# Issuing side work by a running account of engines, banks and buffers in a two-layer decoder trunk

## The chip, the cores and the metric

The kernel runs on one core of a Trainium2 chip. The metric is device time in microseconds (us), the median of three runs. The engines of the core are named as the profile names them: PE is TensorE's matmul, PEld its weight load, DVE is VectorE, ACT is ScalarE, POOL is GpSimd, and SP is SyncE, which here issues every DMA. Each engine works through its own queue in order, and waits for the others by semaphores.

## The reference

The input x is 256 tokens of 2048 channels, float32. Two residual layers, each behind an RMSNorm, are followed by a last RMSNorm.

```
for i in range(2):
    h = rms_norm(x, norm_w[i]); x = x + mixer_i(h)
return rms_norm(x, final_norm_w)
```

Mixer 0 is RWKV-7 time mixing. Six mixtures of h and its shifted copy are made; four go through the 2048 x 8192 projection (r, k, v, gate), two through small low-rank products (decay, learning rate). Each of 32 heads of 64 channels runs a recurrence over the tokens:

```
sa = S @ a_t
S = S * w_t + sa[..., None] * b_t + v_t[..., None] * k_t
y = S @ r_t
```

The result is normalized per head, gets a bonus (the head's sum of r*k*r_k, times v), is multiplied by SiLU of the gate and goes through a 2048 x 2048 output projection. Mixer 1 is differential attention: 16 heads, two causal softmax maps each with a distance penalty, the second subtracted with a learned weight, then values, a per-head RMS norm, the SiLU gate and an output projection.

## The kernel before

**The weight product.** Every projection is a run of `gemm` calls (line 229). A call has 8 steps (4 in the output projections); a step fetches 256 rows of 512 weight columns, splits them into a high half (`high`, a cast on ScalarE, `whi`) and the rest (`low`, a subtraction on VectorE, `wlo`), and multiplies three ways into two banks tagged `gm`. The split of a block is issued three steps ahead (LEAD). There are 320 such steps, in one written order: k, r, v, gate, output of the first layer, then the four projections of the attention layer in four groups, then its output. A layer's k, r, v and gate take 32 steps each; group j of a path is four pairs of heads.

**The side streams.** Everything else is written as Python generators that run while the kernel is built. After each step of the product, `gemm` calls `pump` (line 123), which first issues the waiting DRAM stores and then asks each live stream, in order of rank, for its next piece. A stream yields a price, an estimate of VectorE time. `pump` takes the next piece if VectorE's estimated lead over TensorE plus the price is within the rank's limit (`LIMITS`, line 37; the clocks are kept at lines 84 to 107). A negative price means that more pieces may be taken in the same call. `pump(True)` takes them regardless; it is called where the product can't go on without a stream (`until`, line 151). The order of issue is fixed when the program is built.

The streams of the first layer and their ranks are: scans 0; mixing, low-rank products, gates and `turns` 1; queries 2; keys 3; inverses 4; posts 5.

- `keys` (line 411) makes, for each of 16 pairs of heads, decays and scaled keys in bank `ka`, stores them to DRAM (`ppd`, `ard`, `bkd`) and builds a triangular block per chunk of 64 tokens. Each block takes two steps; the loads of the next are in one of them.
- `inverse` (line 486) inverts these blocks for two groups at once, with a long run of VectorE work (eight 32x32 transposes of 128x1024, 62 pairs of small instructions) and then four pieces of matmuls in banks `qa`.
- `query` (line 551) is called for each pair of heads, with its four chunks. It loads `rt`, `ppr`, `bkq` and `ard`, multiplies (VectorE), makes the score blocks in two `qa` banks and masks them (`G`, VectorE), then transposes in a third use of `qa` (copied out by ScalarE, line 588) and takes the bonus sums in a fourth. There are NR = 6 buffers for its results (`cont`, `G`); the first six run ahead and the others wait until the group that used the buffer is through (`C` marks).
- `scans` (line 610) walks 16 chunks (4 groups of 4) of all heads of a group: the copies `xsc` (lines 654, 655), a product with the inverse in bank `us` and the scaled result `uv` (VectorE), the state's update in `xy`, and the outputs in `ka`, copied by line 697. It needs the queries of the whole group (`Q` mark), the inverse of its pair of groups (`I`) and the values (`v`).
- `posts` (line 725) normalizes the outputs of a group, adds the bonus and applies the gate, on VectorE and some ScalarE. `turns` (line 781) transposes the result in `ka` for the output product.

The first output product starts behind `until("C3")` (line 916), the last chunk's copies; the second half of the output product needs the last `turns` (`until("T3")`, line 913).

## Time and profile before

| | us |
|---|---|
| median of 3 runs (1153.09 to 1157.58) | 1155.38 |
| the profiled execution | 1159.65 |
| its span | 1157.5 |
| PE busy | 1127.8 (97%) |
| DVE busy | 801.4 (69%) |
| ACT busy | 616.6 (53%) |

The first layer takes the span up to about 625 us, the attention layer the rest. A busy matmul row doesn't say that TensorE works at its peak, since matmuls overlap and their ends are modelled. So the profile is read by what TensorE waited for and by the length of a step of the product. A step is 12 matmuls of 512 columns or 24 of 256. Idle time of the other engines matters only where TensorE waits for them.

### The profile page before, as it was taken

What the parts mean: (1) busy time and instruction counts of PE and PEld (TensorE: products, weight loads), DVE (VectorE), ACT (ScalarE), POOL (GpSimd) and SP (SyncE); (2) the same over time, 40 slices, a digit from 0 to 9 for tenths busy, and PEclk for the clock granted to TensorE, in tenths of its full rate; (3) what the DMA queues carried; (4) which work ended last, traced back from release to release, by engine and by line L of the source; (5) the groups of instructions that cost most, each with busy time, mean ns of one, the idle gap of its engine ahead of it and who ended that gap; (6) DMA issues with size and microseconds to landing.
All of it is one profiled execution on the core that took longest, in us unless ns stands there. A gap on an engine that the chain in (4) does not pass through costs nothing.

```text
span 1157.5 us, 21930 instructions
## 1 busy us (share of the span) xinstructions
PE 1127.8 (97%) x8778; PEld 980.3 (85%) x8778; DVE 801.4 (69%) x1316; ACT 616.6 (53%) x1032; POOL 15.0 (1%) x38
## 2 busy tenths in 40 slices
PE   8999998999999989999999999999999999999996
PEld 6999998998777778877878899899889889987885
DVE  5755888988699668787796664476456647646764
ACT  7655854566543465455544543455456455545643
POOL 1010000000000000000001000000000000000000
PEclk9999999999999899999999999999999999999999
DMA  8646768876466557666575566655655665664463
GB/s 261 193 153 200 217 186 247 252 209 202 146 188 199 173 156 228 204 195 176 174 283 179 183 191 190 189 145 149 215 157 154 192 172 146 184 196 148 154 228 109
DMA packets 140823, 217.67 MB, mean 188 GB/s; under 512 B 29793, under 2 KB 45490, under 8 KB 140722
## 3 DMA queue, kind: packets, MB, share of 16 engines
q1 hardware_dynamic: 140722, 216.28, 62.1%
q8 instruction: 69, 1.13, 0.4%
q14 instruction: 32, 0.26, 0.1%
HBM read 197.37 MB, written 18.87 MB: 187 GB/s over the span
## 4 chain that ended last, share of the span: by engine, by line
PE 82%; DVE 9%; DMA 4%; issue 2%; ACT 2%; SPq 1%; ACTq 0%; DVEq 0%
PE gm L103 55%; PE us L103 14%; PE ka L103 7%; PE qa L103 4%; DVE wlo L95 3%; DVE itmp L95 1%; PE qa L107 1%; DVE wp L95 1%; DVE zp L95 1%; DMA wraw<-in_rwkv_w_out_dram 1%; DMA rd<-ev 1%; DMA bkq<-bkd 1%; DMA xin<-in_x_dram 1%; DMA uv<-vdr 1%; PE ka L107 1%
## 5 line engine op out<-in xcount | busy, mean ns | idle before, releaser
L95 DVE TENSOR_TENSOR wlo<-wraw,whi 128x1024 fp32r<-128x1024 f32 x320 | 389.1, 1222 | 118.2 <-ACT whi L196 117.5
L196 ACT CAST whi<-wraw 128x1024 fp32r<-128x1024 f32 x320 | 333.4, 1044 | 201.2 <-PE gm L103 136.1
L103 PE MATMUL gm<-whi,xs 128*128 128x512 f32 x944 | 324.4, 408 | 1.9 <-DVE acc L95 1.1
L103 PE MATMUL gm<-xs,whi 128*128 128x256 f32 x1376 | 256.3, 286 | 0.0
L103 PEld LDWEIGHTS gm<-whi,xs 128*128 128x128 f32 x944 | 180.2, 191 | 45.6 <-ACT whi L196 1.1
L103 PEld LDWEIGHTS gm<-xs,whi 128*128 128x128 f32 x1376 | 214.0, 189 | 3.5 <-issue 1.3
L103 PE MATMUL gm<-xs,wlo 128*128 128x256 f32 x688 | 194.8, 283 | 0.5 <-DVE wlo L95 0.5
L103 PE MATMUL gm<-wlo,xs 128*128 128x512 f32 x472 | 187.1, 396 | 0.0
L103 PEld LDWEIGHTS gm<-xs,wlo 128*128 128x128 f32 x688 | 129.6, 188 | 0.9 <-DVE wlo L95 0.9
L103 PEld LDWEIGHTS gm<-wlo,xs 128*128 128x128 f32 x472 | 90.5, 192 | 18.7
L103 PE MATMUL gm<-xt,whi 128*128 128x256 f32 x352 | 64.2, 283 | 0.0
L103 PE MATMUL gm<-whi,xt 128*128 128x512 f32 x176 | 58.1, 390 | 0.0
L103 PEld LDWEIGHTS gm<-xt,whi 128*128 128x128 f32 x352 | 53.7, 188 | 1.3 <-issue 1.3
L103 PE MATMUL gm<-xt,wlo 128*128 128x256 f32 x176 | 49.3, 280 | 0.0
L103 PEld LDWEIGHTS gm<-whi,xt 128*128 128x128 f32 x176 | 33.0, 188 | 7.6
L993 ACT ACTIVATE sc<-sc,mxx 128x128 f32<-128x128 f32 (+1 forms) x64 | 28.4, 445 | 18.1 <-DVE mxx L95 18.1
L103 PE MATMUL gm<-wlo,xt 128*128 128x512 f32 x88 | 34.7, 394 | 0.0
L95 DVE TENSOR_TENSOR xs<-ev,xs 128x512 fp32r<-128x512 f32 x32 | 22.1, 689 | 16.2 <-ACT xs L326 15.7
L103 PEld LDWEIGHTS gm<-xt,wlo 128*128 128x128 f32 x176 | 33.1, 188 | 0.0
L697 ACT COPY uv<-ka 64x512 f32<-64x512 f32 x16 | 9.3, 581 | 44.4 <-PE ka L103 44.4
L95 DVE SCALAR_TENSOR_TENSOR ev<-big,par,ev 128x256 f32<-128x256 f32 x64 | 28.0, 480 | 6.1 <-ACT ev L314 6.1
L314 ACT ACTIVATE ev<-big,omu 128x256 f32<-128x256 f32 x64 | 29.1, 502 | 5.8 <-DMA rd<-ev 3.9
(265 smaller groups left out, 1662.7 us busy)
## 6 DMA issues: line engine op xcount, KB each, us to landing
wraw<-in_rwkv_w_in_dram SPq DMA_DIRECT2D x128, 512.0 KB
wraw<-in_diff_w_in_dram SPq DMA_DIRECT2D x128, 512.0 KB
wraw<-in_rwkv_w_out_dram SPq DMA_DIRECT2D x32, 512.0 KB
wraw<-in_diff_w_out_dram SPq DMA_DIRECT2D x32, 512.0 KB
bkd<-bkc SPq DMA_DIRECT2D x16, 256.0 KB
bkq<-bkd SPq DMA_DIRECT2D x16, 256.0 KB
xin<-in_x_dram SPq DMA_DIRECT2D x4, 512.0 KB
kd<-ev SPq DMA_DIRECT2D x8, 256.0 KB
```

The source lines that it names most:

```text
L95: return fn(*args, **kw)
L103: PE.matmul(out, lhsT, rhs, start=start, stop=stop, **kw)
L107: PE.transpose(out=out, in_=in_, identity=identity)
L196: A.copy(his[i], raws[i])
L314: A.activation(m, ht[:, k, 1:T + 1], AF.Copy, scale=omu[:, col:col + 1])
L697: A.copy(ye, xyv[64:128].rearrange("p q h n -> p (q h n)"))
L993: A.activation(sc[:, m, b0:b1], sc[:, m, b0:b1], AF.Exp, bias=mx[:, t, m:m + 1], accum_out=sm[:, t, m:m + 1])
```

## The change

The two estimated clocks are replaced by an account (`given`) that follows PE, DVE, ACT, the SP queue and the DMA engines through every instruction as it is issued. It knows which part of which buffer each instruction reads and writes and when, by estimated durations, so an instruction starts in the account when its engine is free and its inputs are there and its output's former readers are done. Two DMAs that depend on each other through DRAM are not made to wait for each other. ACT and DVE instructions have new estimates, a 32x32 transpose 2.03 us.

A stream's next piece is issued only if everything that its last piece gave to other engines is due by TensorE's time plus `SLACK` (1 us), unless the price is negative. A piece may also name banks (`Ask`); their readers must be done by then too. Queries and scans name theirs. The limits become 8 for ranks 0 and 1, 6 for queries and posts, 5 for keys and inverses.

A query is made for one chunk of all four pairs of heads of a group, instead of one pair with its four chunks. Its loads take 64 tokens from each of four DRAM blocks. `r_k` moves from the product on VectorE into a small table `indk`. A scan chunk waits for its own query (`q` mark), and a query for the scan chunk that used its buffer six queries ago (`c` mark).

The post stage of a group may start while that of the group before is still under way, with buffers for two; the scale and shift are loaded once the group before is done.

```diff
+SLACK = 1.0
 BANKS = {"gm": 2, "ka": 2, "qa": 2, "xy": 1, "us": 1}
 LEAD = 3
 RAW = 4
 NR = 6
-LIMITS = (9, 9, 3, 4, 2.5, 3)
+LIMITS = (8, 8, 6, 5, 5, 6)
...
+    def after(table, k, box, eng, t):
+        for other, by, end in table.get(k, ()):
+            if by != eng and meets(box, other):
+                t = max(t, end + 0.07)
+        return t
+
+    def given(eng, cost, outs, ins):
+        t = free["sp" if eng == "dma" else eng]
+        outs, ins = [part(a) for a in outs] , [part(a) for a in ins]
+        for k, box in ins:
+            t = after(wrote, k, box, eng, t)
+        for k, box in outs:
+            t = after(seen, k, box, eng, after(wrote, k, box, eng, t))
+        if eng == "dma":
+            free["sp"] = t + 0.35
+            n = outs[0][1] if outs[0][1][1] > 1 else ins[0][1]
+            t = max(free["sp"] + 1.6, free["dma"])
+            cost = (n[1] - n[0]) * (n[3] - n[2]) * 4 / 240e3
+        end = t + cost
+        free[eng] = end
+        for k, box in outs:
+            wrote[k] = [w for w in wrote.get(k, ()) if not covers(box, w[0])] + [(box, eng, end)]
+            seen[k] = [r for r in seen.get(k, ()) if not covers(box, r[0])]
+        for k, box in ins:
+            seen[k] = [r for r in seen.get(k, ()) if not (r[1] == eng and covers(box, r[0]))] + [(box, eng, end)]
+        if eng != "pe":
+            late[0] = max(late[0], end)
...
+    V = Engine(nc.vector, "dve", 0.155, 0.00104)
+    A = Engine(nc.scalar, "act", 0.2, 0.00082)
+
+    class Queue:
+        def dma_start(self, dst, src):
+            given("dma", 0.0, [dst], [src])
+            nc.sync.dma_start(dst, src)
+
+    DMA = Queue()
...
     def mm(out, lhsT, rhs, start, stop, **kw):
-        n = math.prod(rhs.shape[1:]) * (1.0 if rhs.dtype == F32R else 4.0) / 2400
-        clock["pe"] += max(0.055, n)
+        n = math.prod(rhs.shape[1:])
+        if rhs.dtype == F32R:
+            cost = 0.231 * n / 512 if n > 256 else 0.118
+        else:
+            big_ = lhsT.shape[0] * math.prod(lhsT.shape[1:])
+            cost = 0.042 if big_ <= 1024 else 0.075 if big_ <= 8192 and n <= 64 else max(0.43 * n / 256, 0.21 if big_ > 8192 else 0.166)
+        given("pe", cost, [out], [lhsT, rhs])
         PE.matmul(out, lhsT, rhs, start=start, stop=stop, **kw)
...
+    class Ask(float):
+
+        def __new__(cls, price, *banks):
+            a = float.__new__(cls, price)
+            a.banks = banks
+            return a
+
+    def bank_free(tag, n):
+        k = turns_.get(tag, -1) + 1 + n
+        return max([0.0] + [end for _, by, end in seen.get((tag, k % BANKS[tag]), ()) if by != "pe"])
+
+    def timely(s):
+        if s[2] < 0:
+            return True
+        t = s[3]
+        banks = getattr(s[2], "banks", ())
+        for i, tag in enumerate(banks):
+            t = max(t, bank_free(tag, banks[:i].count(tag)))
+        return t <= free["pe"] + SLACK
+
+    def pump(any_=False):
         for dst, src, name in stores:
             DMA.dma_start(dst, src)
             done.add(name or "")
         stores.clear()
         for s in list(live):
-            while free or max(0.0, clock["dve"] - clock["pe"]) + abs(s[2]) <= LIMITS[s[0]]:
+            while any_ or (timely(s) and max(0.0, free["dve"] - free["pe"]) + abs(s[2]) <= LIMITS[s[0]]):
+                late[0] = 0.0
                 s[2] = next(s[1], None)
+                s[3] = late[0]
                 if s[2] is None:
                     live.remove(s)
                 if s[2] is None or s[2] >= 0:
...
+            asked = [c for c in price if c is not None]
+            yield Ask(sum(asked), *[b for c in asked for b in getattr(c, "banks", ())])
...
+    def query(j, c):
+        g, n = gs[j], j * NCH + c
+        if c == 0:
             g["G"], g["cont"] = [], []
             g["bon"] = L([P, NT, NPG, 2], "bon", 4)
-        rt = L([P, T], "rt", 1)
-        DMA.dma_start(rt, rd[j][q])
-        ppr = L([P, T], "ppr", 1)
-        DMA.dma_start(ppr, ppd[j][q])
-        bkc = L([P, NCH, 2, C], "bkq", 2)
-        DMA.dma_start(bkc.rearrange("p c e t -> p (c e t)"), bkd[j][q])
-        slot = b % NR
-        place, tag, n = (Y, "cont2", NR - 5) if slot > 4 else (S, "acc", 4) if slot else (L, "cont", 1)
-        cont = place([P, 2, NCH, P], tag, n)
-        ar = cont[:, 0].rearrange("p c (a t) -> p c a t", a=2)
-        DMA.dma_start(ar[:, :, 0, :], ard[j][q].rearrange("p (c t) -> p c t", c=NCH))
+        cs = slice(c * C, (c + 1) * C)
+        rt = L([P, NPG, C], "rt", 1)
+        DMA.dma_start(rt, rd[j][:, :, cs].rearrange("q p t -> p q t"))
+        ppr = L([P, NPG, C], "ppr", 1)
+        DMA.dma_start(ppr, ppd[j][:, :, cs].rearrange("q p t -> p q t"))
+        bkc = L([P, NPG, 2, C], "bkq", 2)
+        DMA.dma_start(bkc.rearrange("p q e t -> p q (e t)"),
+                      bkd[j][:, :, c * P:(c + 1) * P].rearrange("q p t -> p q t"))
...
+        V.tensor_tensor(ar[:, :, 1, :], rt, ppr, op=ALU.mult)
+        pr = L([P, NPG, C], "pr", 1)
+        V.tensor_tensor(pr, ar[:, :, 1, :], bkc[:, :, 1, :], op=ALU.mult)
+        yield Ask(1.5, "qa", "qa")
...
+        yield Ask(0.2, "qa", "qa")
         tp = I("qa")
...
+        s = slice(64 * (c % 2), 64 * (c % 2) + 64)
+        for q in range(NPG):
+            mm(bps[s, 2 * q:2 * q + 2], pr[:, q], indk[:, NPG * j + q, :], start=True, stop=True)
+        V.tensor_copy(g["bon"][s, c // 2], bps[s, 0:2 * NPG].rearrange("p (q h) -> p q h", h=2))
         g["G"].append(gm_)
         g["cont"].append(cont)
-        if q == NPG - 1:
-            done.add(f"Q{j}")
+        done.add(f"q{n}")
...
+        def ready(n):
+            return done.issuperset({f"r{n // NCH}", f"K{n // NCH}"} | ({f"c{n - NR}"} if n >= NR else set())
+                                   | ({"keys"} if n == 5 else set()))
+
+        yield from staggered([query(n // NCH, n % NCH) for n in range(NCH * NG)], ready, 2)
...
-            yield from need(f"v{j}", f"Q{j}", f"I{j - j % 2}")
+            yield from need(f"v{j}", f"q{n}", f"I{j - j % 2}")
...
+            yield Ask(1, "us")
...
+            yield Ask(1, "xy", "ka")
+            done.add(f"c{n}")
...
+    def post(j, room):
+        yg, vg = room["y"][j % 2], room["v"][j % 2]
+        DMA.dma_start(yg, yd[j].rearrange("(t p) c -> p t c", p=P))
+        DMA.dma_start(vg, vdr[j].rearrange("(t p) c -> p t c", p=P))
+        yield 1.6
+        mn = L([P, NT, 8], "mn", 2)
+        vr = L([P, NT, 8], "vr", 2)
...
+        yield from need(*([f"P{j - 1}"] if j else []))
+        lnwb = L([P, 2, 512], "wp")
+        for i, w in enumerate((ln_w, ln_b)):
+            DMA.dma_start(lnwb[:, i], w[0:1, 512 * j:512 * j + 512].broadcast_to([P, 512]))
...
+        yield from need("I2", "S0")
+        a, b = L([P, 2, NT, 512], "ws"), L([P, 2, NT, 512], "zf", 2)
+        room = {"y": (a[:, 0], b[:, 0]), "v": (L([P, NT, 512], "zp"), b[:, 1]), "q": a[:, 1]}
+
+        def ready(j):
+            return done.issuperset({f"S{j}"} | ({f"P{j - 2}"} if j > 1 else set()))
+
+        yield from staggered([post(j, room) for j in range(NG)], ready, 1)
...
+    indk = S([P, KT, 2], "indk")
...
+        V.tensor_tensor(indk, ind.unsqueeze(1).broadcast_to([P, KT, 2]), rkc.unsqueeze(2).broadcast_to([P, KT, 2]), op=ALU.mult)
```

## Rows read from the trace of the kernel before

**Rows 1.** The page's first line: span and instructions.

```profile
span 1157.5 us, 21930 instructions
```

**Rows 2.** Busy time by stretch: length, PE, PEld, DVE, ACT, POOL, clock, DMA.

```profile
159.00:256.00 97.00, 93.58 (x975) 89.23 (x972) 87.08 (x187) 50.31 (x90) 0.00 (x0) 1.00 0.75 217
382.00:429.00 47.00, 41.98 (x613) 34.56 (x611) 27.63 (x48) 25.95 (x47) 0.00 (x0) 0.89 0.52 151
630.00:1050.00 420.00, 420.00 (x2701) 375.38 (x2700) 244.31 (x353) 212.10 (x356) 0.00 (x0) 1.00 0.60 176
290.20:293.70 3.50, 3.50 (x10) 2.56 (x8) 3.46 (x5) 0.35 (x1) 0.00 (x0) 0.51 0.36 89
```

**Rows 3.** Whom TensorE waited for: total us, times, longest.

```profile
PE qa L103 <- DVE G L95: 2.6, 1, 2.6
PE qa L103 <- DVE rns L95: 2.4, 1, 2.4
PE qa L103 <- ACT acc L588: 2.1, 2, 1.8
...
PE ka L107 <- ACT uv L697: 2.0, 2, 1.4
PE ka L103 <- DVE bkc L95: 1.6, 2, 1.1
...
PE qa L107 <- DVE G L95: 1.5, 1, 1.5
PE ka L103 <- DVE uv L95: 1.1, 1, 1.1
...
PE gm L103 <- DVE wlo L95: 0.9, 3, 0.4
```

**Rows 4.** Timeline at the first query: start, us, what, idle before it.

```profile
183.32 0.42 DVE L95 TENSOR_TENSOR cont<-rt,ppr 128x256 f32<-128x256 f32 x1 [1.39 <-DMA ppr<-ppd]
...
185.19 1.00 PEld L103 LDWEIGHTS qa<-cont,bkq 64*128 64x128 f32 x16 [2.56 <-DVE pr L95]
```

**Rows 5.** Timeline at the second inverse.

```profile
407.90 1.09 PEld L103 LDWEIGHTS qa<-zp,zf 32*32 32x32 f32 x64 [2.76 <-DVE G L95]
```

**Rows 6.** Chain that ended last, in order of time: start, us, what.

```profile
289.53 4.45 PE gm L103 x12
295.10 2.98 PE gm L103 x12
...
366.46 4.03 PE gm L103 x12
...
398.25 5.11 PE gm L103 x12
409.10 4.54 PE gm L103 x12
```

**Rows 7.** Timeline at the first two and the last scan chunk.

```profile
319.91 0.37 ACT L654 COPY xsc<-ka 64x256 f32<-64x256 f32 x1 [2.83 <-PE ka L103]
...
332.12 0.37 ACT L654 COPY xsc<-ka 64x256 f32<-64x256 f32 x1 [2.30 <-PE ka L103]
...
566.08 0.48 PE L103 MATMUL gm<-whi,xs 128*128 128x512 f32 x1
...
566.41 0.37 ACT L654 COPY xsc<-ka 64x256 f32<-64x256 f32 x1 [0.36 <-PE ka L103]
```

**Rows 8.** Groups by line and shape: busy us, mean ns after the bar.

```profile
L95 DVE TENSOR_TENSOR wlo<-wraw,whi 128x1024 fp32r<-128x1024 f32 x320 | 389.1, 1222 | 118.2 <-ACT whi L196 117.5
...
L95 DVE STREAM_TRANSPOSE wp<-ws 32x1024 f32<-32x1024 f32 x8 | 16.3, 2032 | 0.8 <-PE qa L103 0.6
...
L95 DVE TENSOR_TENSOR uv<-us,rns 64x256 f32<-64x256 f32 x32 | 13.5, 421 | 14.2 <-PE us L103 13.6
...
L95 DVE TENSOR_TENSOR sd<-xy,sd 64x256 f32<-64x256 f32 x16 | 6.8, 422 | 4.3 <-PE xy L103 4.1
```

**Rows 9.** The page's line on DMA packets.

```profile
DMA packets 140823, 217.67 MB, mean 188 GB/s; under 512 B 29793, under 2 KB 45490, under 8 KB 140722
```

More of the change, by code (lines that the diff above doesn't have):

```diff
@@ L76, in I, with part @@
         uid[0] += 1
-        return psp.tile([P, 512], F32, name=f"{tag}_{uid[0]}", tag=tag, bufs=BANKS[tag])
-    PE, DMA = nc.tensor, nc.sync
-    A = nc.scalar
-    clock = {"pe": 0.0, "dve": 0.0}
-    class Vector:
+        return place(psp.tile([P, 512], F32, name=f"{tag}_{uid[0]}", tag=tag, bufs=BANKS[tag]), tag, BANKS[tag])
+    PE = nc.tensor
+    free = {"pe": 0.0, "dve": 0.0, "act": 0.0, "sp": 0.0, "dma": 0.0}
+    wrote, seen, late = {}, {}, [0.0]
+    def part(ap):
+        dims = list(ap.ap)
+        if str(ap.space).endswith("DRAM"):
+            return ap.name, (0, 1, ap.offset, ap.offset + 1 + sum((n - 1) * st for st, n in dims), None)
+        row = rows_[ap.name]
+        lo, p0 = ap.offset % row, ap.offset // row
+        at = {lo}
+        if math.prod(n for st, n in dims[1:]) <= 32:
+            for st, n in dims[1:]:
+                at = {o + i * st for o in at for i in range(n)}
+        else:
+            at = None
+        return slots[ap.name], (p0, p0 + dims[0][1], lo, lo + 1 + sum((n - 1) * st for st, n in dims[1:]), at)
@@ new lines, in meets, with covers @@
+    def meets(a, b):
+        return (a[0] < b[1] and b[0] < a[1] and a[2] < b[3] and b[2] < a[3]
+                and (a[4] is None or b[4] is None or bool(a[4] & b[4])))
+    def covers(a, b):
+        return (a[0] <= b[0] and a[1] >= b[1] and a[2] <= b[2] and a[3] >= b[3]
+                and (a[4] is None or b[4] is not None and a[4] >= b[4]))
+    def after(table, k, box, eng, t):
[3 more added lines that the diff above has]
+        return t
@@ L87, in __getattr__, with __init__ @@
+    class Engine:
+        def __init__(self, ns, eng, base, rate):
+            self.ns, self.eng, self.base, self.rate = ns, eng, base, rate
         def __getattr__(self, op):
-            fn = getattr(nc.vector, op)
+            fn = getattr(self.ns, op)
             def issue(*args, **kw):
                 dst = args[0] if args else kw["out"]
-                src = [a for a in args[1:3] if hasattr(a, "shape")] + ([kw["in_"]] if "in_" in kw else [])
+                rest = list(args[1:]) + [v for k, v in kw.items() if k not in ("out", "accum_out")]
+                src = [a for a in rest if hasattr(a, "shape")]
@@ L105, in transpose @@
     def transpose(out, in_, identity):
-        clock["pe"] += 0.215
+        given("pe", 0.109, [out], [in_])
         PE.transpose(out=out, in_=in_, identity=identity)
@@ new lines, in query @@
+        cs = slice(c * C, (c + 1) * C)
[6 more added lines that the diff above has]
+                      bkd[j][:, :, c * P:(c + 1) * P].rearrange("q p t -> p q t"))
+        slot = n % NR
+        where, tag, k = (Y, "cont2", NR - 5) if slot > 4 else (S, "acc", 4) if slot else (L, "cont", 1)
@@ new lines, in post, with heads @@
+    def post(j, room):
[5 more added lines that the diff above has]
+        vr = L([P, NT, 8], "vr", 2)
+        def heads(ap):
+            return ap.rearrange("p (h n) -> p h n", h=8)
+        for t in range(NT):
+            y = yg[:, t]
+            V.tensor_reduce(mn[:, t], heads(y), axis=AX.X, op=ALU.add)
+            V.tensor_scalar(mn[:, t], mn[:, t], 1.0 / 64, None, op0=ALU.mult)
+            V.tensor_tensor(heads(y), heads(y), bc_heads(mn[:, t]), op=ALU.subtract)
+            yield 1.6 if t == 0 else 0.7
+        sqs = []
+        for t in range(NT):
+            sqs.append(room["q"][:, t])
+            A.activation(sqs[t], yg[:, t], AF.Square)
+            v = vg[:, t]
+            V.tensor_tensor(heads(v), heads(v), bc_heads(gs[j]["bon"][:, t].rearrange("p q h -> p (q h)")),
+                            op=ALU.mult)
+            if t == 0:
+                yield 1.4
+            else:
+                V.tensor_reduce(vr[:, 0], heads(sqs[0]), axis=AX.X, op=ALU.add)
+        yield from need(*([f"P{j - 1}"] if j else []))
+        lnwb = L([P, 2, 512], "wp")
+        for i, w in enumerate((ln_w, ln_b)):
+            DMA.dma_start(lnwb[:, i], w[0:1, 512 * j:512 * j + 512].broadcast_to([P, 512]))
+        yield 0.7
+        V.tensor_reduce(vr[:, 1], heads(sqs[1]), axis=AX.X, op=ALU.add)
+        yield 1.4
+        A.activation(vr, vr, AF.Sqrt, bias=eps[:, 1:2], scale=1.0 / 64)
+        for t in range(NT):
+            V.tensor_tensor(vg[:, t], vg[:, t], lnwb[:, 1], op=ALU.add)
+        yield 1.6
+        V.reciprocal(vr, vr)
+        for t in range(NT):
+            y = yg[:, t]
+            V.tensor_tensor(heads(y), heads(y), bc_heads(vr[:, t]), op=ALU.mult)
+            V.tensor_tensor(y, y, lnwb[:, 0], op=ALU.mult)
+            yield 1.4
+        yield from need(f"g{j}")
+        for t in range(NT):
+            y, gt = yg[:, t], ys["pw"][:, j, t]
+            V.tensor_tensor(y, y, vg[:, t], op=ALU.add)
+            V.tensor_tensor(gt, y, gt, op=ALU.mult)
+            if t == 0:
+                yield 1.4
+        done.add(f"P{j}")
```

122 lines of the change are left out of this document (34 added, 88 removed).

## The prediction

> **What bounds the kernel now.** I read the page first, then busy time by stretch, then what TensorE waited for, then single hand-overs. The page gives TensorE busy nearly all the way through a span of 1157.5 us [rows 1]. The stretches say where it is not: from 630 to 1050 us, nearly the whole attention layer, it is busy for all 420 us, while the 47 us from 382 to 429 lack 5 us and ran at a granted clock of 0.89 [rows 2]. So the order of TensorE's own work is the bound, and what a new order can return is only the holes and what the clock lost after them. The change leaves the weight product (the two projections of each layer) and nearly all side matmuls as they are.
>
> The list of TensorE's waits is the whole purse [rows 3]. Eight of its rows belong to the first layer's side streams: 2.6, 2.4, 2.1, 2.0, 1.6, 1.5, 1.1 and 0.9, together 14.2 us. In front of the weight loads the same holes are 0.2 to 0.4 us longer, as [rows 4, 5] show; I use the matmuls' column. The clock adds to it: four product groups that follow such holes took 4.45, 4.03, 5.11 and 4.54 us where the usual group takes 2.98 [rows 6]. That is 1.47 + 1.05 + 2.13 + 1.56 = 6.2 us. The granted clock after the first of them was 0.51, the lower level of 1.2 GHz [rows 2]. So at most 14.2 + 6.2 = 20.4 us can be saved.
>
> How a hole is made is seen at 183 us [rows 4]. VectorE reaches the first instruction of a query and waits 1.39 us for its load, holds up everything queued behind it (the key stream's decay and `bkc` products), and TensorE's weight load for the query waits 2.56 us.
>
> **The change, part by part.** The sum is made against the profiled execution, 1159.65 us with its 1157.5 us span. The runs' median, 1155.38, lies 4.3 us below; a saving in the one is carried to the other unchanged.
>
> *The account's gate (timely).* A stream's next step is issued only when what its last step gave to other engines, its loads included, is due by TensorE's time plus 1 us. A hole falls away where the late thing is the stream's own earlier step. That holds for four rows of [rows 3]: the query after its loads (DVE rns 2.4, the hole of [rows 4]), the key stream after its `bkc` product (1.6), the query's transposes after its masked product (DVE G on L107, 1.5), the scan after its `uv` product (1.1): 6.6 us. Two of them were followed by a slow group (1.47 and 1.05), 2.5 us. What hides a refused step is the next weight-product step of some 2.9 us, which is there from start to end of the layer; without it (rival A) each refusal would stand bare. Saved: 9.1 us.
>
> *What the gate doesn't see.* The inverse takes `qa` banks and `turns` takes `ka` banks without naming them in an Ask, so both can still run into a bank that another stream's evacuation holds. These are DVE G before an inverse matmul (2.6), ACT acc L588 before one (2.1) and ACT uv L697 before a turn (2.0): 6.7 us, with 2.13 + 1.56 = 3.7 us of slow groups behind the first two. [rows 5] show one: the inverse's weight load waits 2.76 us for the masked product G. New is the pace. Queries ran in a burst there, two steps apart, so every step touched `qa`; by chunk they follow the scan, whose clean chunk takes three steps, so one step in three leaves `qa` alone. I take a third of the inverse's 8.4 us, 2.8 us, and none of the turns' 2.0. The bounds are the whole 10.4 saved, and 8.4 more lost: the limits for queries and inverse double (3 to 6, 2.5 to 5), so G may stand deeper in VectorE's queue when the inverse meets it.
>
> *The slack of 1 us.* The gate lets TensorE arrive up to 1 us early. Sixteen chunks with three scan steps, sixteen queries with two and sixteen key blocks with two make 112 steps that hand to TensorE. Bounds are 0 and, every tenth late by the full microsecond, 11 us. In the trace one of the sixteen `uv` hand-overs shows a wait of over half a microsecond (1.1, [rows 3]). One in sixteen of 112 at half a microsecond each is 3.5 us, which I take as lost.
>
> *Deeper VectorE backlog.* The low half of a weight (`wlo`, 1.22 us [rows 8]) stands behind the side work in VectorE's queue and is needed two product steps after its issue, 5.6 to 6 us where no side work lies between (a group is 2.98 at most undisturbed [rows 6]). With a backlog of 5 us it ends at 6.2, 0.2 to 0.6 us late. Today such waits cost 0.9 us [rows 3], at the inverse's first 32x32 transposes, priced at some 1.2 and taking 2.03 [rows 8]; the new account prices them right while the limit doubles. I take no difference; bounds -0.9 and +5 us (0.3 us for each of sixteen steps).
>
> *Queries by chunk.* Matmuls and VectorE instructions keep their number. The bonus product is 4 matmuls with 64 columns of weights instead of 2 with 128, about equal. `pr` becomes a plain product like the one that takes 0.42 us [rows 4]; it lies beside other work. The four loads keep their bytes, 640 KB a query, but `rt`, `ppr` and `bkq` now come in pieces of 256, 256 and 512 bytes. The queue has 29793 packets under 512 B already [rows 9] and was 0.75 busy where the queries start [rows 2], so I take 0, with the rival below. Scan chunk n now waits for query n, and query n+6 for chunk n, where whole groups waited before. This moves the scan: the first chunks start at 319.91 and 332.12, 12.2 us apart, the last of the sixteen at 566.41 [rows 7], so 15 intervals took 246.5 us where 15 x 12.2 = 183 would do. But the product that needs the scan's end starts at 566.08, at the same moment [rows 7]. TensorE wasn't waiting, so an earlier scan saves 0; it buys 63 us of room.
>
> *Post stage, `indk`, second layer.* Two posts at once cost no new TensorE work; their VectorE work lies beside products, and the earlier scan gives them time. `indk` is one small instruction in the preparation. In the attention layer the gate may refuse a step where the residual's additions crowd VectorE; every group but the last has 32 steps for the 16 parts of its stream, and the last has 16 with its last part empty and the transposes before it still coverable by the next product. I take 0.
>
> Sum: -9.1 - 2.8 + 3.5 = -8.4, so 1151.3 against the profiled execution and **1147 us** against the median.
>
> **The rivals.**
>
> *A, the scans come too late (slower).* Every scan, query and key step can be refused, and a step that issues loads counts their landing as its own. The key stream (two product steps a block, loads in one of them) may need three, the second inverse then ends later, and half of the scan waits for it. From the decisive point on, an average above 16.4 us a chunk (246.5/15; one refusal a chunk, 12.2 + 3 = 15.2, still fits), the first output product meets an unfinished scan and issues streams with no product to hide them. At two and a half, 12.2 + 7.5 = 19.7 us, 15 x 3.3 = 50 us or 2.5 chunks are left over. Each bares two copies (0.37 each, [rows 7]), two `uv` and four state instructions (0.42 each [rows 8]), 3.3 us, so 8.2; the last post, some 10 steps priced 1.3 to 1.6 in the code, is bared too, 15 us; two or three slow groups of 1.5 add 4. With 8.4 saved before, that is 1155.4 - 8.4 + 27 = **1174**. For it: VectorE was busy for 87 of the 97 us from 159 to 256 [rows 2]. Against it: 63 us of room.
>
> *B, the holes only move.* The inverse still meets the queries, and slack and backlog cost 4 us more than I took: -9.1 + 3.5 + 4 = -1.6, about **1154**.
>
> *C, late loads.* [rows 4] show a load not yet landed holding VectorE 1.39 us and TensorE 2.56. The account counts bytes only; if the smaller pieces land that much later, half of the sixteen queries would bring such a hole, 8 x 2.56 = 20.5: 1155.4 - 8.4 + 20.5 = **1168**. The page "DMA: Bandwidth & Descriptors" of the Trainium skill, Specifications, asks for at least 512 B a transfer and says that below it the engine reads, modifies and writes; 256-byte pieces would suffer by it, and no row here shows their time by itself.
>
> *D, all holes go,* the inverse's too: -20.4, **1135**.
>
> **How the numbers follow.** Forecast 0.60 (own range 1138 to 1158), B 0.17, A 0.13, C 0.05, D 0.05. About 0.5% (5.8 us, so 1149.6 and 1161.2) is what a measurement can tell from no change. Faster: 0.78 of the forecast's 0.60, 0.05 of D and some of B, 0.52. Slower: A, most of C, a part of B and of the forecast's upper end, 0.24. The rest, 0.24, is the same. The range goes from 1132, below D, to 1168, so that most of A and little else is left out.
>
> **What would show it.** Right: no row DVE rns or bkc in TensorE's waits; the copies `xsc` of the sixteen chunks 12 to 15 us apart and the last well before 560; a granted clock of 1.0 but for one or two windows, at the inverse's matmuls. Wrong: TensorE waits on `wlo`, many waits of 0.3 to 1 us at `uv`, `G` or `xsc` (slack); for A holes at the first output product and a last `xsc` after it; for C VectorE waiting on `rt`, `ppr` or `bkq`.

## The result, and the profile after

The changed kernel takes **1143.97 us** (median of 4 runs, 1142.93 to 1144.91); the kernel before took 1154.93 beside it. The ratio is 0.9891 [0.9873, 0.9909], 11.0 us less; the forecast was 1147. In the profiled executions the span went from 1157.5 to 1142.6 us, 14.9 less: the profiled execution of before lies 4.7 us above that median, the one of the changed kernel 0.8. The experiments were timed in three later comparisons, in which the kernel before took 1155.79, 1156.71 and 1155.29; a difference between kernels of two comparisons is uncertain by up to 2 us.

The page of the changed kernel, the span, TensorE's busy time and the DMA packets [rows 1, 9]:

```profile
span 1142.6 us, 22076 instructions
...
PE 1121.1 (98%) x8842; PEld 974.1 (85%) x8842; DVE 800.1 (70%) x1317; ACT 616.7 (54%) x1032; POOL 15.0 (1%) x38
...
DMA packets 159255, 217.67 MB, mean 191 GB/s; under 512 B 46177, under 2 KB 65970, under 8 KB 159154
```

Whom TensorE waited for in it (total us, times, longest), the answer to [rows 3]. All instructions of a helper now have its line, so one goes by the tiles:

```profile
PE xy L191 <- DMA prm<-in_rwkv_mu_dram: 2.6, 1, 2.6
PE gm L187 <- DVE wlo L166: 2.3, 4, 1.5
PE gm L187 <- DVE acc L166: 2.0, 1, 2.0
PE ka L187 <- DVE rsd L166: 1.7, 1, 1.7
PE ka L191 <- ACT uv L166: 1.3, 2, 0.7
PE qa L187 <- DVE G L166: 1.3, 1, 1.3
PE us L187 <- POOL zb L367: 1.1, 1, 1.1
PE qa L187 <- DVE bon L166: 0.3, 1, 0.3
PE qa L187 <- ACT acc L166: 0.2, 1, 0.2
PE gm L187 <- ACT ev L166: 0.2, 1, 0.2
```

The reader is to see what is missing: `rns`, `bkc`, the transposes behind `G` and the scan behind `uv`, the four rows on which the gate's term rested. The whole list fell from 20.8 to 13.0 us. One row of some size grew beside `wlo`: `acc`, VectorE's addition of the output product's results, from 1.1 us in two waits to 2.0 in one. Busy time by stretch (length, PE, PEld, DVE, ACT, POOL, clock, DMA, GB/s), two of the stretches of [rows 2], and two more:

```profile
290.20:293.70 3.50, 3.50 (x32) 2.76 (x31) 2.21 (x4) 0.21 (x1) 0.00 (x0) 1.00 0.69 205
382.00:429.00 47.00, 45.48 (x521) 36.66 (x522) 39.15 (x62) 25.19 (x42) 0.00 (x0) 0.96 0.68 186
425.00:428.40 3.40, 3.40 (x10) 2.58 (x8) 0.00 (x0) 1.49 (x2) 0.00 (x0) 0.51 0.00 0
564.90:568.30 3.40, 3.40 (x10) 2.65 (x9) 3.33 (x7) 0.00 (x0) 0.00 (x0) 0.50 0.47 163
```

The stretch from 382 to 429 lacks 1.5 us instead of 5. Between 30 us and the end the lower clock of 1.2 GHz is left in two places: behind the second inverse, where the next product step took 4.53 us in the chain that ended last, and in the fifth step of the output product, 4.41 from its start to the next step's, which begins behind the hole at `acc`. From the chain and the timeline:

```profile
424.23 4.53 PE gm L187 x12
...
564.46 0.47 PE L187 MATMUL gm<-whi,xs 128*128 128x512 f32 x1 [1.97 <-DVE acc L166]
```

Against 2.98 the two steps lose 3.0 us, where there were 6.2 [rows 6]. Waits and slow steps together give 7.8 + 3.2 = 11.0 us of the spans' 14.9. That this is also the medians' difference is chance, since all these rows are of the profiled executions. Of the 3.9 us left, an estimated 1.9 can be the clock too: the kernel before had four stretches near 0.5 (at 290, 365, 396 and 410 us), together 17.1 us, the changed kernel two, together 6.8; half of the difference is 5.1 us, and the product steps alone account for 3.2. The rest is not assigned to rows.

The first and the last of the sixteen scan copies and the first output product, in the timeline [rows 7]:

```profile
318.50 0.76 ACT L166 COPY xsc<-ka 64x256 f32<-64x256 f32 x2 [1.53 <-PE ka L187]
...
542.90 0.76 ACT L166 COPY xsc<-ka 64x256 f32<-64x256 f32 x2 [2.21 <-PE ka L187]
...
550.19 0.51 PE L187 MATMUL gm<-whi,xs 128*128 128x512 f32 x1
```

The last chunk is 23.5 us earlier, but the output product is 16 us earlier too: only 7 us lie between them. This room decides most of the experiments. A table by stage, read from the starts of the product's steps in each profile (us; the first three columns are points in time; "drain" is the time between the last step of the gate's projection and the first output product, in which only side work is issued; "first" is the span up to the first output product, drain included, "out" the output product, "att" the rest):

| kernel | last key block | second inverse | last scan copy | drain | first | out | att | median of runs |
|---|---|---|---|---|---|---|---|---|
| before | 257 | 418 | 566.8 | 0.8 | 566.1 | 97.2 | 494.2 | 1154.9 |
| changed | 303 | 439 | 543.3 | 1.2 | 550.2 | 97.7 | 494.7 | 1144.0 |
| queries by pair, old posts | 297 | 437 | 575.5 | 38.4 | 575.3 | 99.0 | 494.7 | 1171.0 |
| old account, queries by chunk | 260 | 437 | 533.0 | 0.0 | 561.2 | 100.1 | 494.4 | 1155.7 |
| gate open | 296 | 431 | 537.3 | 0.4 | 566.3 | 95.5 | 494.3 | 1159.6 |
| old limits | 292 | 515 | 579.9 | 70.9 | 579.0 | 98.4 | 494.6 | 1175.4 |
| slack 0 | 335 | 467 | 573.2 | 30.8 | 572.5 | 97.6 | 500.3 | 1173.2 |
| transposes at 2.1 | 297 | 462 | 556.1 | 15.0 | 555.3 | 98.0 | 494.7 | 1151.4 |
| slack 0, transposes at 2.1, banks named | 326 | 492 | 575.4 | 47.3 | 574.7 | 97.2 | 500.1 | 1174.2 |
| old posts | 301 | 438 | 547.1 | 1.2 | 546.8 | 107.3 | 494.7 | 1150.7 |
| slack 0, loads ahead not counted | 301 | 456 | 551.8 | 5.1 | 551.6 | 98.4 | 501.2 | 1154.2 |
| slack 1.2 | 302 | 411 | 541.7 | 0.8 | 562.4 | 93.3 | 494.4 | 1148.7 |
| three edits, banks 0.25 | 283 | 450 | 544.7 | 1.2 | 551.9 | 95.7 | 494.7 | 1144.3 |
| three edits, banks 0.5 | 295 | 440 | 532.3 | 0.0 | 545.5 | 95.7 | 494.7 | 1137.7 |

The change's whole gain is in "first". Where a stream is too late, it shows as a drain.

### The profile page after: what moved, and what is told of

It is laid out like the page before. It is cut to its first block, busy times and chain, and to the rows that moved or that the text cites. A ratio compares the mean times of both kernels' runs of the same rounds, so it can differ in the third digit from the quotient of the medians.

```text
span 1142.6 us, 22076 instructions
## 1 busy us (share of the span) xinstructions
PE 1121.1 (98%) x8842; PEld 974.1 (85%) x8842; DVE 800.1 (70%) x1317; ACT 616.7 (54%) x1032; POOL 15.0 (1%) x38
## 2 busy tenths in 40 slices
DMA packets 159255, 217.67 MB, mean 191 GB/s; under 512 B 46177, under 2 KB 65970, under 8 KB 159154
## 3 DMA queue, kind: packets, MB, share of 16 engines
q1 hardware_dynamic: 159154, 216.28, 63.5%
## 4 chain that ended last, share of the span: by engine, by line
PE 90%; DVE 5%; DMA 2%; ACT 1%; issue 1%; SPq 0%; ACTq 0%; DVEq 0%
PE gm L187 61%; PE us L187 15%; PE ka L187 7%; PE qa L187 4%; DVE wlo L166 2%; PE qa L191 1%; DMA wraw<-in_rwkv_w_in_dram 1%; PE ka L191 1%; DMA xin<-in_x_dram 1%; PE xy L187 1%; DVE wp L166 1%; DVE zf L166 0%; DVE itmp L166 0%; PE xy L191 0%; DVE G L166 0%
## 5 line engine op out<-in xcount | busy, mean ns | idle before, releaser
L187 PE MATMUL gm<-whi,xs 128*128 128x512 f32 x944 | 320.2, 405 | 2.0 <-DVE acc L166 2.0
L166 ACT ACTIVATE sc<-sc,mxx 128x128 f32<-128x128 f32 (+1 forms) x64 | 28.4, 446 | 17.1 <-DVE mxx L166 17.1
L166 ACT ACTIVATE th<-ka 128x256 f32<-128x256 f32 (+1 forms) x32 | 12.3, 384 | 33.0 <-PE ka L187 33.0
```

What stands on the lines that cost most here:

```text
L166: return fn(*args, **kw)
L187: PE.matmul(out, lhsT, rhs, start=start, stop=stop, **kw)
```

## The experiments

**The parts alone.** Three kernels put one old part into the changed kernel (gate open, old limits, old posts), one puts two into it (old queries and old posts), and one a new part into the old.

The account, its gate and the new limits, but queries by pair of heads, scans behind whole groups, posts one after the other:

```diff
-    def query(j, c):
+    def query(j, q):
-            yield from need(f"v{j}", f"q{n}", f"I{j - j % 2}")
+            yield from need(f"v{j}", f"Q{j}", f"I{j - j % 2}")
...
```

> The changed kernel with its account, gate, banks and limits, but with the queries made by pair of heads, the group marks and the post stage of the kernel before: the account alone. Theory (the gate on a stream's own late results is what saves; chunks only give the scan room): the four guarded rows (DVE rns, bkc, G before the transposes, uv; 6.6 us and 2.5 us of slow groups) go here too, so 1145 to 1149 us, with the last chunk's xsc copy near 550 to 566 us. Rival (the chunks save, by doing away with the waits of whole groups): 1152 to 1156 us. Rival (a bounded forecast of the scan's lateness): with whole groups and refused steps the scan misses the first output product, over 1158 us.

Measured: 1171.04 us, ratio 1.0137 [1.0107, 1.0167]. The gate's projection ended at 536.9 us, 12 us earlier than in the changed kernel, but then 38.4 us were drained: the last queries came at 547 us, the last four scan chunks 8 us apart between 551 and 575, at a granted clock of 0.62 from 540 to 576. The gate without the queries by chunk and the new posts is rival A. `rns` and `bkc` are gone from its waits; `uv` (3.9) and the transposes' `G` (1.1) are not.

Queries by chunk in the kernel before, all else as it was:

```diff
-    def query(j, q):
+    def query(j, c):
-            yield from need(f"v{j}", f"Q{j}", f"I{j - j % 2}")
+            yield from need(f"v{j}", f"q{n}", f"I{j - j % 2}")
...
```

> The kernel before, with its two clocks, limits and posts, but with queries made by chunk and the marks by chunk: the chunks alone. Theory: holes of the guarded kind stay, since nothing refuses a step whose input is late; 1150 to 1158 us, the last xsc copy clearly before 560 us. Rival (the chunks save): 1142 to 1148 us.

Measured: 1155.65 us, ratio 0.9997 [0.9981, 1.0013]: nothing. The scan ends at 533.0, 28 us ahead of the output product, and holes stay: `rns` 2.5, `bkc` 1.7, and at the second inverse `G` 2.4 and `cont` 1.8. The transposes behind `G` and the scan behind `uv` have no row any more, without any gate. In the profiles the output product begins 4.9 us earlier than in the kernel before, but takes 2.9 us longer, with a wait of 4.0 at `acc`. Room by itself saves nothing in the end, as the prediction said.

The changed kernel with its gate always open:

```diff
     def timely(s):
-        if s[2] < 0:
-            return True
+        return True
```

> The changed kernel with the gate always open: the account still prices VectorE and the limits 8, 8, 6, 5, 5, 6 hold, but no step waits for its own results or for banks. Theory: holes come back, and more of them since the limits are deeper: 1152 to 1165 us, TensorE's waits on VectorE and ScalarE results 15 us or more. Rival (the better durations and the limits save, not the gate): 1142 to 1147 us.

Measured: 1159.62 us, ratio 1.0036 [1.0022, 1.005], 15.6 us above the changed kernel. TensorE's waits in it (some rows), and the matmuls of the second inverse in the timeline:

```profile
PE qa L187 <- DVE G L166: 6.0, 2, 3.9
...
PE ka L187 <- DVE bkc L166: 1.4, 2, 1.1
...
PE qa L187 <- DVE pr L166: 1.0, 1, 1.0
```

```profile
400.65 1.20 PE L187 MATMUL qa<-zp,zf 32*32 32x32 f32 x64 [3.91 <-DVE G L166]
410.09 1.20 PE L187 MATMUL qa<-zf,wp 32*32 32x32 f32 x64 [1.81 <-ACT acc L166]
419.63 1.20 PE L187 MATMUL qa<-zp,zf 32*32 32x32 f32 x64 [2.10 <-DVE G L166]
428.23 1.28 PE L187 MATMUL qa<-zf,wp 32*32 32x32 f32 x64 [1.57 <-ACT cont L166]
```

Holes are back with the gate open, so in this arrangement it is the gate that removes them. But 9.4 us of them stand at the inverse, which the prediction held to be out of the gate's sight; of the four rows that it gave to the gate, only `bkc` (1.4) is back, and `pr` (1.0) where `rns` stood. The gate had room to refuse steps only because the rest was there too.

The changed kernel with the old limits:

```diff
-LIMITS = (8, 8, 6, 5, 5, 6)
+LIMITS = (9, 9, 3, 4, 2.5, 3)
```

> The changed kernel with the limits of the kernel before (9, 9, 3, 4, 2.5, 3). Theory: the gate keeps its 9 us; the waits on wlo (2.3 us in the changed kernel) shrink to under 1, the inverses get slower: 1141 to 1147 us. Rival (the deeper limits save): 1149 us or more, with a later scan.

Measured: 1175.42 us, ratio 1.0176 [1.0148, 1.0203]. Busy time by stretch, columns as above:

```profile
445.00:510.00 65.00, 65.00 (x560) 52.30 (x557) 53.69 (x78) 30.16 (x39) 0.00 (x0) 1.00 0.59 177
510.00:580.00 70.00, 48.38 (x750) 40.95 (x745) 57.17 (x111) 22.27 (x46) 0.00 (x0) 0.72 0.45 111
```

From 13 to 510 us TensorE's list of waits is empty. But the second inverse ended at 515 instead of 439, so eight chunks of the scan lay bare at the end: a drain of 70.9 us, TensorE idle for 22 of the 70 above, at a clock of 0.72.

The posts one after the other, all else as changed:

```diff
-        yield from staggered([post(j, room) for j in range(NG)], ready, 1)
+        for j in range(NG):
+            yield from need(f"S{j}")
...
```

> The changed kernel with the post stages one after the other, as before the change; account, limits and queries by chunk stay as changed. Theory (the prediction gave the post stage 0): 1143 to 1146 us. Rival (a scan that ends only some 7 us ahead of the output product leaves the last posts too little time one after the other, and their steps and the turns are bared before the second half of the output product): 1148 to 1158 us, with holes between 560 and 610 us.

Measured: 1150.68 us, ratio 0.9953 [0.9935, 0.9971], 6.7 us above the changed kernel. TensorE in its timeline, the last post's result `big` in front of the turns, and the stretch behind it:

```profile
607.78 0.44 PE L191 MATMUL ka<-ident,big 128*128 128x128 f32 x1 [4.91 <-DVE big L166]
```

```profile
609.00:612.40 3.40, 3.38 (x11) 2.80 (x12) 1.65 (x3) 2.13 (x3) 1.83 (x6) 0.50 0.00 0
```

The first output product began 3.4 us earlier, but "out" took 107.3 us instead of 97.7. So the new post stage is worth 6.7 us in this arrangement; its new prices and later loads of scale and shift came and went with it.

**The slack.** One number, to 0:

```diff
-SLACK = 1.0
+SLACK = 0.0
```

> The changed kernel with one number changed: a step is issued only when the account has what it waits for done by TensorE's time, with no slack of 1 us. Theory (the slack term of the prediction, +3.5 us, is real): the changed kernel's remaining holes that are 0.3 to 1.5 us long (the second inverse behind G 1.5, two turns of 0.85, some of 0.35 to 0.4) go, together 3 to 4.5 us, and with the inverse's hole the slow group after it (1.5 us): 1138 to 1141 us. Rival (refusing has a price, there are only some 7 us of room between the last scan copy and the first output product): the stricter gate refuses more, the sixteen copies lie over 0.5 us further apart, the scan runs past the first output product and steps are bared: 1148 to 1165 us. No effect: 1143 to 1145.

Measured: 1173.18 us, ratio 1.0148 [1.0123, 1.0174], 29 us above the changed kernel. The key stream ended at 335 us instead of 303, the second inverse at 467 instead of 439, and the drain in front of the output product is 30.8 us long. The projection itself ended at 541.6 us, 7.4 earlier than with the slack, so the strict gate saves time there; what it refused came due at the end. The holes that the theory meant to close, the inverse's `G` (2.2) and the turns' `uv` (1.5), are still in the list of waits. Most of that drain as a stretch:

```profile
545.00:573.00 28.00, 18.67 (x275) 15.57 (x276) 26.16 (x49) 10.63 (x20) 0.00 (x0) 0.76 0.31 88
```

TensorE at the start of that drain, in the timeline:

```profile
547.37 1.50 PE L187 MATMUL us<-xsc,zf 64*64 64x64 f32 x16 [2.88 <-ACT xsc L166]
550.90 1.57 PE L187 MATMUL xy<-uv,cont 128*64 128x64 f32 x16 [2.03 <-DVE uv L166]
```

Which refusals took the room? The key stream's loads for its next block and the scan's loads for its next chunk count as something their next step waits for, though it doesn't read them. With slack 0 still, these were left out of the account's lateness:

```diff
+    def unseen(load, *args):
+        t = late[0]
+        made = load(*args)
+        late[0] = t
+        return made
...
-                    nxt = key_loads((b + 1) // 4, (b + 1) % 4)
+                    nxt = unseen(key_loads, (b + 1) // 4, (b + 1) % 4)
...
-            load_v(n + 1)
+            unseen(load_v, n + 1)
```

> No slack, as in the run without slack (1173.2 us against 1144.0 of the changed kernel in its own comparison), and in addition the loads that a stream issues ahead for its next block or chunk (the key stream's next key block, the scan's next values) no longer count as something its next step waits for. Theory: these refusals, for data that the next step does not read, are what ate the room without slack; with them gone the key stream ends some ten product steps earlier, nearly no step is left for the first output product, and the time comes back to 1142 to 1150 us. Rival: it is the refusals for real operands and banks that cost the room; the loads change little and the time stays at 1165 to 1175 us.

Measured: 1154.23 us, ratio 0.9993 [0.9981, 1.0006]: 19 of the 29 us came back, less than expected. By stage, the first layer is repaired: up to the first output product 551.6 us, 1.4 above the changed kernel, where slack 0 alone had 572.5, and the drain is 5.1 instead of 30.8. What is left is in the attention layer, 501.2 us instead of 494.7, and is in the other two runs with slack 0 as well (500.3, 500.1). TensorE's waits name the larger part of it:

```profile
PE qa L191 <- DVE y L166: 3.5, 2, 1.8
```

These are the last transposes of that layer, at 1092 and 1094 us; the clock behind them was 0.54 from 1096 to 1100 us. So both theories hold a part: refusals for data that nobody reads yet cost the first layer 20.9 us, and a second price of slack 0, in the other layer, I had not seen.

A fifth of a microsecond more:

```diff
-SLACK = 1.0
+SLACK = 1.2
```

> The changed kernel with a slack of 1.2 us in place of 1.0: one number, a fifth of a microsecond. If the slack is a smooth price (each late hand-over costs what it is late), at most some 112 hand-overs are later by 0.2 us and few of them are near the limit: 1143 to 1147 us. Rival (the order is set by which steps happen to be refused, and one step admitted or refused moves all behind it): the holes before the inverse and the bonus products come back with their slow groups and the time goes to 1149 to 1155 us.

Measured: 1148.65 us (1146.64 to 1154.02), ratio 0.9949 [0.9928, 0.997], between the two ranges. The profiled execution, 7.5 us longer in span than the changed kernel's, has these waits:

```profile
PE qa L187 <- DVE G L166: 2.1, 1, 2.1
...
PE qa L187 <- ACT acc L166: 1.6, 1, 1.6
...
PE ka L187 <- DVE bkc L166: 1.2, 1, 1.2
```

One hole behind `G`, one behind `acc` and one behind `bkc` are back, as the rival has it, 4.9 us together; the rows of 0.2 us (`big`, `sd`, `uv`) come to 0.6. This execution lies 3.7 us above the median of its kernel, so part of its length is that execution's own. The second inverse even ended 28 us earlier. The slack acts by which steps it admits more than by a late hand-over each.

**The inverse.** Its transposes take 2.02 us and are priced at 1.1, so two went into one step. Both sets of them are priced at 2.1 here, and the inverse and the turns name their banks. In the changed kernel's timeline, VectorE, and TensorE behind it:

```profile
376.40 4.07 DVE L166 STREAM_TRANSPOSE zf<-zp 32x1024 f32<-32x1024 f32 x2
...
381.78 0.50 PE L187 MATMUL gm<-wlo,xs 128*128 128x512 f32 x1 [1.50 <-DVE wlo L166]
```

```diff
             V.transpose(out=zf[s, :, o:o + 32].rearrange("p c k -> p k c"), in_=zp[s])
-            yield -1.1
+            yield -2.1
...
```

> The changed kernel with the inverse's two sets of 32x32 transposes (2.02 us each) priced at 2.1 instead of 1.1, and with the inverse and the turns naming the banks that they take (which by itself leaves the order of instructions as it is). Theory: the hole in front of a wlo product at 379.9 us (1.66 us; two such transposes in one step, 4.07 us of VectorE) goes, and nothing else moves by more than a step: 1141 to 1143 us. Rival: one transpose a product step puts the second inverse's end later by two or three steps of 3 us, the second half of the scan waits for it and uses up the room of some 7 us: 1146 to 1155 us.

Measured: 1151.44 us, ratio 0.996 [0.9944, 0.9976], 7.5 us above the changed kernel, the rival. The wait at 380 us shrank to 0.3, but the second inverse ended 23 us later, at 462, and the last two chunks of the scan were drained, 15.0 us (`sd` 3.0 us among TensorE's waits).

Both edits, slack 0 and transposes at 2.1 (as in the two diffs), with the banks named:

> Both edits at once: no slack, the inverse's transposes at 2.1, and the banks named by the inverse and the turns. If slack and price each take away the holes that are put down to them and the room holds: 1135 to 1139 us, the best of all. If refusals eat the room: at or above the kernel without slack alone, 1148 to 1170 us.

Measured: 1174.23 us, ratio 1.0156 [1.0132, 1.0181]; inverse at 492, a drain of 47.3 us. The refusals ate the room.

The prediction put the inverse's holes down to banks that it doesn't name. Naming them, with the slack of 1 us, gives the same order of instructions on every engine, and so does dropping the bank test altogether: in the changed kernel the banks of the account refuse no step, and all that its gate does is done by a stream's own late results. With slack 0 the names do matter: unnamed, the inverse meets `G` for 2.2 us; named (and the transposes at 2.1) for nothing. So the gate sees this hole only with a smaller slack for banks. The hole in the changed kernel's timeline, the answer to [rows 5]:

```profile
422.29 1.29 DVE L166 TENSOR_TENSOR G<-qa,mask 128x512 f32<-128x512 f32 x2
423.03 1.09 PEld L187 LDWEIGHTS qa<-zf,wp 32*32 32x32 f32 x64 [1.50 <-DVE G L166]
```

Two kernels have three edits: `unseen` as above, banks named by the inverse and the turns, and a slack of their own for banks:

```diff
-            t = max(t, bank_free(tag, banks[:i].count(tag)))
+            if bank_free(tag, banks[:i].count(tag)) > free["pe"] + BSLACK:
+                return False
...
-                yield 1
+                yield Ask(1, "ka")
...
```

With BSLACK 0.25 and SLACK 1.1:

> The changed kernel with three edits: loads issued ahead don't count for the next step; the inverse's matmul steps and the turns name the banks they take; a bank may be late by 0.25 us only, while a stream's own last step may be late by 1.1 us. Theory (the unguarded inverse and turns of the prediction, reached through a strict bank test): the hole of 1.53 us before the second inverse, its slow group and the two turns of 0.85 us go, some 4 to 5 us, and the earlier key stream pays for the refusals: 1138 to 1143 us. Rival: other hand-overs are late by as much instead, or the inverse is later and the scan's end with it: 1144 to 1152 us.

Measured: 1144.32 us, ratio 0.9896 [0.9876, 0.9917], as the changed kernel.

With BSLACK 0.5 and SLACK 0.9:

> The same three edits with a bank slack of 0.5 us and a slack of 0.9 us for the stream's own step. In the kernel's own account this order ends the first layer 3.4 us before the changed kernel's, the other (0.25 and 1.1) 1.7 us before. Theory: 1138 to 1142 us. Rival: 1144 to 1152 us, as above. If the two differ by more than 4 us, the outcome is a matter of which steps happen to meet, not of the rule.

Measured: **1137.66 us** (1137.1 to 1138.26), ratio 0.9842 [0.9825, 0.9859]: the fastest kernel here, 17.6 us below the one before. TensorE's waits in it, all of them:

```profile
PE xy L192 <- DMA prm<-in_rwkv_mu_dram: 3.3, 1, 3.3
PE gm L188 <- ACT ws L167: 1.7, 1, 1.7
PE ka L188 <- DVE rsd L167: 1.6, 1, 1.6
PE us L188 <- POOL zb L375: 1.1, 1, 1.1
PE gm L188 <- DVE wlo L167: 0.9, 3, 0.5
PE qa L188 <- DVE bon L167: 0.3, 1, 0.3
```

Neither kernel waits for `G` before the inverse any more, as the strict bank test would have it; that this test and not one of the other two edits did it was not run by itself at these slacks. The turns' row (`uv` on `ka`, 1.3) is gone in the second kernel only, though both name the turns' bank. And the two lie 6.7 us apart with the same edits: the first has 3.6 us more of waits, among them new ones at `uv` (1.0 and 0.3 us, at 324 and 352 us) and 1.0 at `wlo` (at 379), and a drain that is 1.2 us longer. That the second met none of these is not the rule's doing, as far as these runs show. Past 30 us the clock of both stayed at 1.00 until the last steps.

## Why the prediction was right, and where it was not

The sign, the place and the main mechanism held: the bound is TensorE's order, the gain is holes and the clock behind them, and 1147 against 1144.0 is within the forecast's own range. That the sum, -8.4, came so near to -11.0 is in part luck. Its terms were off by up to 3.5 us in both directions, and the saving was to carry over from the profiled execution unchanged, where it was 14.9 in the one and 11.0 in the other.

*The gate, -9.1.* The four rows (6.6 us) and the two slow steps behind two of them (2.5) are gone, so the sum is right; that all of it is the gate's is not. Without a gate and with queries by chunk, `rns` and `bkc` stay in the kernel before (2.5 and 1.7), while the rows of the transposes' `G` and the scan's `uv`, which had the slow steps behind them, are gone; with the gate and whole groups it is the other way round (`G` 1.1 and `uv` 3.9, part of it in the drain). So these runs give 4.0 us of the four rows to the gate, and the other 2.6 with their slow steps to the chunks. What the gate is worth beyond that lies at the inverse, next. The term was also written as if it were the gate's alone. With its limits but without the queries by chunk and the new posts it costs 15 us (1171.0 against 1155.8 beside it), and with both but the old limits 20. The prediction's step that failed is the room, "it buys 63 us": it compared the scan's end by chunk at its best pace with the old output product. Chunks without a gate left 28 us; with the gate, refusals moved the key stream's end by 46 us, and the product came nearer. 7 us were left, and the sum holds only there.

*The unguarded inverse, -2.8.* Too small: its rows went from 4.7 us to 1.3 + 0.3 + 0.2 = 1.8, its slow steps from 3.7 to 1.55, so -5.0; the turns went from 2.0 to 1.3, where nothing was taken. The reason given, the slower pace of queries by chunk, was wrong: at that pace and without a gate the second inverse waited 4.6 us with the old limits, as before, and 9.4 with the new. With the gate and whole groups the inverses still waited 3.9. So neither shortens these holes by itself, the two together do, although the inverse names no bank; as I read it, by spacing the queries' steps that fill `qa`.

*The slack, +3.5.* Wrong in kind. The sixteen chunks' `uv`, `G` and `xsc` hand-overs, the 112 steps of the estimate, have no row of a late one among TensorE's waits; the turns (1.3) and the inverse (1.8), counted above, are late, but not through the slack: without it they are late by 1.5 and 2.4, since they name no bank. And without slack the kernel is 29 us slower. The microsecond is not a loss but what keeps the streams in time.

*The VectorE backlog, 0 (-0.9 to +5).* Measured +1.4 (`wlo` 0.9 to 2.3, of which 0.4 and 0.5 lie in the last output product), within the bounds. I wrote that the new account prices the transposes right; it times them at 2.03, but the price that the limit is asked for stayed 1.1. The right price is slower here.

*Queries by chunk, 0.* Right by itself (ratio 0.9997). The smaller pieces cost TensorE nothing that can be seen. Packets under 512 B went from 29793 [rows 9] to 46177, and the queue's share from 62.1 to 63.5%; no row of TensorE's waits is a query's load. One row of VectorE's waits is, by the release that the profile infers, though `wlo` doesn't read that load:

```profile
DVE wlo L166 <- DMA bkq<-bkd: 2.9, 1, 2.9
```

The prediction said that no row shows their time by itself, but the packets in the trace do: a packet of 256 B took a median of 18 ns in both kernels, one of 512 B 27, of 1024 B 46, of 2048 B 84. So the same bytes take 1.7 times as long in pieces of 256 B as in one of 2048 (8 x 18 against 84), and the time of all packets grew from 724 to 731 us for each of the 16 engines on average. The rule of the Trainium skill that stands beside rival C ("DMA: Bandwidth & Descriptors", Specifications) is not borne out here by a loss at TensorE, nor by a step at 512 B: 256 B more take 9 ns, the next 512 take 19 and the next 1024 take 38.

*Posts, 0.* Wrong as a part: they are worth 6.7 us. In the kernel before, one after the other was enough, and no turn waited for `big`; with posts gated and the output product 16 us earlier it isn't. As I read it, a cost that the gate brought and a gain that the posts brought were both left out and cancelled; the gate's share was not run by itself. Nor is "their VectorE work lies beside products" free: the hole of 1.97 us at `acc` stands behind instructions of the posts (`mn`, `zf`) in VectorE's queue, and with its slow step the row costs 2.3 us more than before.

*The attention layer, 0.* Right at this slack (494.2 and 494.7); at slack 0 it is +5.4 to +6.5.

*What would show it.* `rns` and `bkc` gone, two windows at the lower clock, last copy ahead of 560: as written, but only one window is at the inverse. "12 to 15 us apart" was too narrow, 9 to 25 (the eighth came 25 us behind the seventh, the thirteenth 9 behind the twelfth). *Rival A* did not happen, but it is the nearest neighbour: four kernels that differ from this one in one to three places ended at 1171.0, 1173.2, 1174.2 and 1175.4, where its price gave 1174. Its mechanism, a step's loads counted as its own, is what the run with these loads left out shows at slack 0.

Open: which of the admitted steps makes 1.0 better than 1.2, and why the last two kernels differ; 2 to 4 us of the profiled spans' difference.

## What to carry to other kernels

A gate that refuses side work until its operands are due removes holes, but each refusal delays a stream, so find first how much room the streams have before the point that needs them, and buy that room (finer dependences, interleaved stages) in the same change. Let the gate wait only for what the next step reads, not for loads issued ahead (worth 19 us here at slack 0, and not run by itself at 1); see whether each test of the gate refuses anything, since here the one for banks did not; and measure the neighbours of a chosen constant, since in an order that is fixed when the program is built one admitted step moves all behind it. Where parts act on a common room, test them by taking one away from the whole: here the queries by chunk alone were worth nothing, and the gate with its limits alone cost 15 us. The chunk of work left for the point that needs a stream (the drain) is the number to watch.

## What the hardware showed that I had not expected

Holes of the same length don't cost the same. Behind the wait of 1.31 us at the second inverse (1.50 at its weight load) the clock stood at 0.51 for 3.4 us and the next step took 4.53 us; behind the wait of 1.50 for `wlo` at 381.78 it stayed at 1.00 (and in the fastest kernel behind one of 1.70 at 559.36, in the output product):

```profile
381.50:385.00 3.50, 3.22 (x26) 2.45 (x27) 3.47 (x7) 1.65 (x4) 0.00 (x0) 1.00 0.55 149
```

The inverse's transposes of equal size cost differently too. Those that read or write a permuted view (`wp`, `zf`) take 2.02 us, those between plain blocks (`zp<-zf`) 1.23, in the list of groups (busy us, mean ns after the bar):

```profile
L166 DVE STREAM_TRANSPOSE zf<-zp 32x1024 f32<-32x1024 f32 x8 | 16.2, 2020 | 0.2
...
L166 DVE STREAM_TRANSPOSE zp<-zf 32x1024 f32<-32x1024 f32 x4 | 4.9, 1232 | 0.1
```

And loads in pieces of 256 and 512 bytes (16384 more packets under 512 B) left the queue's share of the span nearly as it was, 62.1 and 63.5%; what grew is the issue of some of these loads on SP's queue, `bkq` from a median of 0.42 to 0.51 us and `ppr` from 0.42 to 0.50, while `rt` stayed at 0.47 and 0.46.
